# Feed-forward entry of a two-layer hybrid trunk: order of the first products, banks of the conv taps, a fourth plain tile

## The chip, the cores and the metric

One core of a Trainium2 chip runs the whole program in a single launch. The metric is the device time of that launch in microseconds (us), lower is better. The engines that matter are TensorE (PE in the profile, with its weight loads as PEld), VectorE (DVE), ScalarE (ACT), GpSimd (POOL), and the DMA queue that SyncE issues (SP).

## The reference

Two layers over 512 positions and a width of 1024. Each layer adds a mixer (attention of two kinds) and then a feed-forward part to the residual stream; the change sits at the passage from the mixer to the feed-forward part, in both layers.

```python
x = x + mixer(rms_norm(x, norm_mix[i]))        # nsa_mixer, then swa_mixer
h = rms_norm(x, norm_ffn[i])
a, u = jnp.split(h @ w_gu, 2, axis=-1)          # w_gu: 1024 x 5632
a = causal_depthwise_conv(a, conv_w, conv_b)    # three taps along the sequence
x = x + (jax.nn.silu(a) * u) @ w_down           # w_down: 2816 x 1024
```

## The kernel before, in words

Everything is held transposed: 128 features on the partitions, the 512 positions along the free axis. The width of 1024 is eight such tiles, the inner feed-forward width of 2816 is 22 (index f). To keep fp32 accuracy every operand of a product is split into a high part (a cast to fp32r, on ACT) and a low part (the difference, on DVE or POOL), and a product is high times high, high times low and low times high: 24 matmuls of 512 columns for one 128 x 512 result over a width of 1024.

**Leaving the mixer.** `out_last` (L390 to L432) makes the eight tiles of the last quarter of the output projection. For each tile m it adds the product to the residual stream (L421, DVE), splits the result with `split_x` (L300: `xh[m]` on ACT in L305, `xl[m]` on DVE in L306), and two tiles later adds the square of the tile to the statistics of the norm (ACT L232; the sum in L238 on POOL, for the last tiles on DVE). The gain of the norm is in `xh` and `xl`, the factor 1/rms (`rstd`) is not: products can start before it is known, and it is applied to their results.

**First products.** `first_products` (L282) loads the weights of the gate and the up half of f = 0 (`load_w`, L174: DMA to `wraw`, cast to `wh` on ACT in L182, difference `wl` in L183) and makes both products in two PSUM banks, tags `mm` and `s`. Its steps are of three matmuls: for each k the product of the high weight with `xh[k]`, of the high weight with `xl[k]`, of the low weight with `xh[k]`; all eight k of the gate half come before the up half. `finish_among` (L261) puts the reduction of the statistics (L248, L249), the power on POOL (L254) and the transposes that spread the result (L257) among these steps, by the counts in AMONG_FFN.

**Plain tiles.** `gate_up(f)` (L547) runs for f = 0, 1, 2 (PLAIN is 3). It multiplies the gate product by `rstd` into `apad` (L550), runs the three taps and the silu (`activate`, L533: one ACT and two DVE instructions that accumulate in a PSUM bank `py`, then the silu on ACT), makes the up product, multiplies it by `rstd` (L554, DVE) and by the silu (L555, POOL). The gate product is in a bank of tag `mm`, the up product and `py` in banks of tag `s`. There are two banks of `mm`, two of `s`, three of `t` (transposes, and copies that serve as PSUM sources) and one of `o`. The list PLO names the plain halves whose `wl` is made on POOL, by the number 2f + j (j is 0 for gate, 1 for up); the others use DVE.

**Seven-product tiles.** f from the number of plain tiles on is made by `gate_up_7(f)` (L612): a 2 x 2 scheme with seven products of half the columns and half the width (84 matmuls of 256 columns) in place of eight (which is 96). It wants sums and differences of quarters: of the weights (`weights`, L587: four sums on POOL in L596, seven casts on ACT in L602, five copies to `t` banks in L606, seven differences on DVE in L608), made per f, and of the activations (`operands(i)`, L564, for i = 0 to 3), made once per layer into `xs`. One `operands(i)` is two DVE multiplications by the gain and `rstd` (L569), four POOL sums (L573 to L576), four casts on ACT (L579), three copies to `t` banks on ACT (L583) and four differences on DVE (L585). The smallest of the four pieces, `x1l` with 256 columns, has no copy: its difference reads SBUF twice. OPER says after which plain tile each `operands(i)` stands in the program.

**What sets the order.** The program is written tile by tile, and the framework's scheduler puts the instructions of each engine in one order by their place in the program (which is their priority) and by when its own model expects them to be ready; a tag with n buffers is given out in the order of the program. Each engine then runs its list in that order. Weight loads all issue on SP. `issue_after` holds a block of instructions behind one named instruction on the same engine.

Of the kernel before, what the change touches and what calls it, by code (L numbers as in the profile page):

```python
# [11 lines left out]
F32 = mybir.dt.float32  # L12
F32R = mybir.dt.float32r
AF = mybir.ActivationFunctionType
ALU = mybir.AluOpType
AX = mybir.AxisListType

P = 128
T = 512
NT = T // P  # L20
DM = 1024
NK = DM // P
# [9 lines left out]
B_MM, B_S, B_T, B_O = 2, 2, 3, 1  # L32
# [12 lines left out]
LAST = (("mm", "mm", "s", "s", "mm", "mm", "s", "s"),) * 2  # L45
HALVES = slice(0, T // 2), slice(T // 2, T)
STATS_LAG = 2
FULL_NSA = (0, 3)
FULL_SWA = (0, 1, 2, 3, 7)
OUT_ORDER = (6, 2, 0, 1, 7, 3, 4, 5)  # L50
# [4 lines left out]
RATE_NSA = (4.2, 2.8, 1.5, 2.2)  # L55
AMONG_FFN = ((11, 2, 1), (11, 2, 1))
STATS_DVE = (5, 5)
PLAIN = (3, 3)
OPER = ((0, 1, 1, 1), (0, 1, 1, 1))
PLO = ((3, 6, 7), (3, 6))  # L60
BUFS = dict(a1=2, a2=2, u1=2, u2=2, s1=2, s4=2, ha1=2, la1=2, ha2=1, la2=1, hs1=1, ls1=1, hs4=1, ls4=1, hu2=1, lu2=1)
GL = [n for n in ("u1", "a1", "u2", "a2", "s1", "s4", "ha1", "la1", "ha2", "la2", "hs1", "ls1", "hs4", "ls4") for _ in range(BUFS[n])]
BANKS = (0, 1, 3, 5, 4)
# [6 lines left out]
def run(steps):  # L70
    for _ in steps:
        pass
# [67 lines left out]
def trunk(ctx: ExitStack, tc: tile.TileContext, x, w_nsa, w_gate, w_c1, w_c2, w_nsao, w_nsao3, w_swa, w_swao,  # L140
          w_swao3, w_gu, w_dn, consts, tables, vecs, convs, pe, swa_vb, out):
    nc = tc.nc
# [5 lines left out]
    ps = ctx.enter_context(tc.tile_pool(name="ps", bufs=2, space=PSUM))  # L148
# [8 lines left out]
    V = VecIndex(vec)  # L157
# [5 lines left out]
    xh = [cp.tile([P, T], F32R, name=f"xh{k}", tag=f"xh{k}") for k in range(NK)]  # L163
    xl = [cp.tile([P, T], F32R, name=f"xl{k}", tag=f"xl{k}") for k in range(NK)]
# [3 lines left out]
    def f32(t):  # L168
        return t.bitcast(F32)
# [112 lines left out]
    def first_products(layer, stats):  # L282

        ws = [chunks(load_w(w_gu[layer, j, 0], DM, nc.vector), NK) for j in range(2)]
        pts = [ps.tile([P, T], F32, name=n, tag=n, bufs=b) for n, b in (("mm", B_MM), ("s", B_S))]

        def steps():
            for pt, w in zip(pts, ws):
                for k in range(NK):
                    nc.tensor.matmul(pt, w[k][0], xh[k], start=k == 0, stop=False)  # L290
                    nc.tensor.matmul(pt, w[k][0], xl[k], start=False, stop=False)
                    nc.tensor.matmul(pt, w[k][1], xh[k], start=False, stop=k == NK - 1)
                    yield

        s = steps()
        stats.finish_among(s, AMONG_FFN[layer][:2], after=AMONG_FFN[layer][2])
        run(s)
        return pts

    def split_x(xt, k, gain, eng=None):  # L300
        g = V(gain, k)
        if eng is nc.vector:
            ins = nc.vector.tensor_scalar(xh[k], xt, g, None, op0=ALU.mult)
        else:
            ins = nc.scalar.activation(xh[k], xt, AF.Copy, scale=g)  # L305
        nc.vector.scalar_tensor_tensor(xl[k], xt, g, f32(xh[k]), op0=ALU.mult, op1=ALU.subtract)  # L306
        return ins


    def evacuate(pool, pt):  # L310
# [79 lines left out]
    def out_last(out, src, gain, stats, layer):  # L390

        early, (oh, ol) = EARLY[layer], out
        ws, pts = [], {}

        def product(m, c, n, lo, cols=slice(0, T), first=False, last=False):
            o = c * 4 * P + m % 4 * P
            nc.tensor.matmul(pts[m][:, cols], ws[m // 4][n][:, o:o + P], (ol if lo else oh)[:, c, cols],
                             start=first, stop=last)

        def products_0(m):  # L400
            if m % 4 == 0:
                ws.append(next_w())
            tag = LAST[layer][m]
            pts[m] = ps.tile([P, T], F32, name=tag, tag=tag, bufs={"mm": B_MM, "s": B_S, "t": B_T}[tag])
            product(m, 0, 0, 0, first=True)
            product(m, 0, 1, 0)
            product(m, 0, 0, 1)

        for m in range(early):
            products_0(m)  # L410
        for cols in HALVES:
            for m in range(early):
                product(m, 1, 0, 0, cols)
                product(m, 1, 1, 0, cols)
        for m in range(NK):
            if m >= early:
                products_0(m)
                product(m, 1, 0, 0)
                product(m, 1, 1, 0)
            product(m, 1, 0, 1, last=True)  # L420
            nc.vector.tensor_tensor(X[m], pts.pop(m), src[m], op=ALU.add)  # L421
            ins = split_x(X[m], m, gain)
            if m >= STATS_LAG:
                if m - STATS_LAG >= STATS_DVE[layer]:
                    stats.eng = nc.vector
                with tc.issue_after(ins.ins):
                    stats.add(X[m - STATS_LAG], m - STATS_LAG)
        with tc.issue_after(ins.ins):
            for m in range(NK - STATS_LAG, NK):
                if m >= STATS_DVE[layer]:  # L430
                    stats.eng = nc.vector
                stats.add(X[m], m)  # L432

    def out_weights(wa, gs):
        n = 2 * len(gs) * P
# [17 lines left out]
    X, Xt = [None] * NK, [None]  # L453
# [52 lines left out]
def ffn(tc, layer, e):  # L506
    nc, wp, ps, V = e["nc"], e["wp"], e["ps"], e["V"]
    rstd, X, load_w, mm3, proj = e["rstd"], e["X"], e["load_w"], e["mm3"], e["proj"]
    f32, Stats, residual = e["f32"], e["Stats"], e["residual"]
    e["lo_eng"][0] = nc.vector  # L510
    H = T // 2
    with tc.tile_pool(name=f"ffn{layer}", bufs=1) as pool:
# [7 lines left out]
        g, x_tags = {}, [(x, k) for x in ("xh", "xl") for k in range(NK)]  # L520
# [9 lines left out]
        for t in apad:  # L530
            nc.vector.memset(t[:, 0:2], 0.0)

        def activate(f, a):  # L533
            y = pool.tile([P, T], F32, name="y", tag="y", bufs=1)
            py = ps.tile([P, T], F32, name="s", tag="s", bufs=B_S)
            nc.scalar.activation(py, a[:, 2:], AF.Identity, scale=conv(f * 3 + 2), bias=conv(3 * NF + f))
            nc.vector.scalar_tensor_tensor(py, a[:, 1:T + 1], conv(f * 3 + 1), py, op0=ALU.mult, op1=ALU.add)
            nc.vector.scalar_tensor_tensor(py, a[:, 0:T], conv(f * 3), py, op0=ALU.mult, op1=ALU.add)
            nc.scalar.activation(y, py, AF.Silu)
            return y  # L540
# [6 lines left out]
        def gate_up(f):  # L547
            pa = plain(f, 0, "mm") if f else e["first"][0]
            a = apad[f % 2]
            nc.vector.tensor_tensor(a[:, 2:], pa, rstd, op=ALU.mult)  # L550
            y = activate(f, a)
            pu = plain(f, 1, "s") if f else e["first"][1]
            u = gated(f)
            nc.vector.tensor_tensor(u, pu, rstd, op=ALU.mult)  # L554
            nc.gpsimd.tensor_tensor(u, u, y, op=ALU.mult)  # L555
# [3 lines left out]
        xs = pool.tile([P, 7, NK // 2, 2, H], F32R, name="xs")  # L559
# [4 lines left out]
        def operands(i):  # L564
            n = [half(t, F32) for t in (("ha2", "hs4"), ("la2", "ls4"))[i % 2]]
            t = [half(t, F32).rearrange("p (o t) -> p o t", o=2) for t in (("hs1", "hu2"), ("ls1", "lu2"))[i % 2]]
            for h in range(2):
                k = i + h * NK // 2
                nc.vector.scalar_tensor_tensor(n[h], X[k], V(f"ffn{layer}", k), prs, op0=ALU.mult, op1=ALU.mult)  # L569
            x1l, x1r, x2l, x2r = (n[h][:, c] for h in range(2) for c in HALVES)  # L570
            t2, t1, t3, t4 = (t[j][:, h] for j in range(2) for h in range(2))
            eng = nc.gpsimd
            eng.tensor_tensor(t1, x1r, x1l, op=ALU.subtract)  # L573
            eng.tensor_tensor(t3, x2r, x1r, op=ALU.subtract)
            eng.tensor_tensor(t2, x2r, t1, op=ALU.subtract)
            eng.tensor_tensor(t4, x2l, t2, op=ALU.subtract)  # L576
            for o, src in ((slice(0, 1), x1l.unsqueeze(1)), (slice(5, 7), n[1].rearrange("p (o t) -> p o t", o=2)),
                           (slice(1, 3), t[0]), (slice(3, 5), t[1])):
                nc.scalar.copy(xs[:, o, i, 0], src)  # L579
                if o.stop - o.start == 2:  # L580

                    src2 = ps.tile([P, T], F32, name="t", tag="t", bufs=B_T).rearrange("p (o t) -> p o t", o=2)
                    nc.scalar.copy(src2, src)  # L583
                    src = src2
                nc.vector.tensor_tensor(xs[:, o, i, 1], src, f32(xs[:, o, i, 0]), op=ALU.subtract)  # L585

        def weights(f):  # L587
# [23 lines left out]
        def gate_up_7(f, cue):  # L611
            ws = weights(f)  # L612
# [12 lines left out]
            a, u = apad[f % 2], gated(f)  # L625
# [20 lines left out]
            product(pc, 4)  # L646
            add(ul, pc, ul)
            cue(6)
            nc.gpsimd.tensor_tensor(u, u, activate(f, a), op=ALU.mult)

        prs = ps.tile([P, T], F32, name="o", tag="o", bufs=B_O)
        nc.scalar.copy(prs, rstd)
        for f in range(PLAIN[layer]):
            gate_up(f)
# [35 lines left out]
        gain = "mix1" if layer == 0 else None  # L690
# [37 lines left out]
        ins = down(last, halves[1])  # L728
# [5 lines left out]
def nsa(tc, e):  # L734
# [55 lines left out]
    vc = pool.tile([P, 2, P], F32R, name="vc")  # L790
    NV = 4 if max(FULL_NSA, default=0) > 3 else 2
    vcd = pool.tile([P, NV, 2, P], F32R, name="vcd")
# [187 lines left out]
    def head(g, r, fill):  # L980
        q, kk, v2 = qs[g], keys[g], vs[g]
        h = 4 * g + r
        full = h // 2 in FULL_NSA
        pts, acc = {}, []
# [580 lines left out]
```

## Time and profile before

| what | us |
|---|---|
| three timed runs, median (lowest to highest) | 1279.53 (1273.96 to 1279.56) |
| the profiled execution, its own time | 1280.34 |
| its span from first to last instruction | 1278.6 |
| PE busy / DVE / ACT / POOL in the span | 1220.3 / 906.8 / 797.4 / 580.0 |

The profiled execution lies 0.8 us above the median of the timed runs, and 1.7 us of it are outside the span. A row of the timeline has the start, the time from the start to the end of the merged instructions, the engine, the line, the operation, the tiles (out<-in), the shape and the count; a bracket is the engine's idle time just before it and what ended it. A matmul's own duration overlaps the next one's, so a pace is read from starts. The granted clock (PEclk) is a share of full speed.

### The profile page before, as it was taken

To read this page: it belongs to the slowest core of one execution; us is meant where nothing else is said; L and a number is where in the kernel's file an instruction comes from. 1 tells how busy PE (TensorE), PEld (TensorE's weight loads), DVE (VectorE), ACT (ScalarE), POOL (GpSimd) and SP (SyncE) were. 2 spreads that over 40 slices of the span, in tenths; PEclk is the share of its full clock that TensorE was granted. 3 is DMA by queue.
4 is the path that set the end of the run, shared out by engine and by line. 5 is a ranking of instruction groups with operands and counts; after the bars stand their busy time and mean duration, and the time that the engine had idled before them with its cause. 6 is when DMAs were issued, how large, how long until landed. Compare 5 with 4: busy or idle time off the path is not lost.

```text
span 1278.6 us, 20545 instructions
## 1 busy us (share of the span) xinstructions
PE 1220.3 (95%) x7246; PEld 1055.7 (83%) x7246; DVE 906.8 (71%) x1799; ACT 797.4 (62%) x1660; POOL 580.0 (45%) x451
## 2 busy tenths in 40 slices
PE   7999999989998999999999998999889999999997
PEld 5867886777876999999888886778679999998886
DVE  6466777878678888889533367997888788893223
ACT  4377677867549888878422225865687888873222
POOL 4485544533239666764000136322576766620002
PEclk9999999989999999999999999999999999999998
DMA  5746645041122333331233355323423333213323
GB/s 188 229 148 203 195 128 151 30 144 38 49 90 96 116 103 101 106 108 54 85 96 91 107 162 158 111 80 92 133 74 101 99 100 107 87 61 98 100 91 124
DMA packets 66486, 141.71 MB, mean 111 GB/s; under 512 B 8528, under 2 KB 16976, under 8 KB 66384
## 3 DMA queue, kind: packets, MB, share of 16 engines
q1 hardware_dynamic: 65008, 139.25, 35.2%
q8 instruction: 57, 0.93, 0.3%
q10 hardware_dynamic: 1376, 1.15, 0.3%
q14 instruction: 45, 0.37, 0.1%
HBM read 123.14 MB, written 17.24 MB: 110 GB/s over the span
## 4 chain that ended last, share of the span: by engine, by line
PE 67%; DVE 13%; POOL 6%; DMA 5%; issue 5%; ACT 2%; SPq 1%; POOLq 0%; DVEq 0%; ACTq 0%
PE mm L205 29%; PE mm L619 11%; PE s L619 8%; PE o L619 7%; PE s L1165 2%; PE o L1007 1%; PE t L1189 1%; DVE ls L608 1%; PE o L1307 1%; DVE xl L306 1%; DMA q<-d 1%; DMA d<-rh 1%; DVE p L1184 1%; PE t L1409 1%; DMA d<-rl 1%
## 5 line engine op out<-in xcount | busy, mean ns | idle before, releaser
L182 ACT CAST wh<-wraw 128x1024 fp32r<-128x1024 f32 (+3 forms) x132 | 122.2, 926 | 234.9 <-PE mm L205 142.9
L183 DVE TENSOR_TENSOR wl<-wraw,wh 128x1024 fp32r<-128x1024 f32 (+3 forms) x80 | 100.0, 1253 | 115.6 <-PE mm L205 74.8
L183 POOL TENSOR_TENSOR wl<-wraw,wh 128x1024 fp32r<-128x1024 f32 (+3 forms) x52 | 99.0, 1906 | 135.0 <-PE mm L205 67.5
L205 PE MATMUL mm<-xs,wh 128*128 128x512 f32 (+1 forms) x374 | 141.7, 383 | 1.6 <-DVE apad L623 1.6
L238 POOL TENSOR_TENSOR rt<-rt 128x512 f32<-128x512 f32 x22 | 31.5, 1431 | 198.2 <-ACT rt L232 198.0
L205 PE MATMUL mm<-xh,wh 128*128 128x512 f32 x248 | 104.4, 423 | 12.3 <-ACT wh L182 11.3
L205 PE MATMUL mm<-xl,wh 128*128 128x512 f32 x248 | 101.8, 412 | 2.6 <-DVE xl L306 2.6
L608 DVE TENSOR_TENSOR ls<-s,hs 128x512 fp32r<-128x512 f32 x76 | 89.9, 1190 | 3.1 <-ACT hs L602 1.9
L205 PE MATMUL mm<-xs,wl 128*128 128x512 f32 (+1 forms) x374 | 90.9, 382 | 0.0
L619 PE MATMUL o<-xs,ha 128*128 128x256 f32 x608 | 87.2, 287 | 2.2 <-DVE ls L569 1.7
L619 PE MATMUL mm<-xs,hs 128*128 128x256 f32 x608 | 87.8, 283 | 0.3 <-DVE apad L623 0.3
L596 POOL TENSOR_TENSOR s<-u,u 128x512 f32<-128x512 f32 x38 | 51.7, 1361 | 78.6 <-DMA u<-in_w_gu 58.6
L205 PEld LDWEIGHTS mm<-xs,wh 128*128 128x128 f32 x374 | 70.3, 188 | 17.0 <-DVE apad L623 2.0
L1175 ACT ACTIVATE p<-p,sm 128x128 f32<-128x128 f32 (+3 forms) x128 | 71.7, 562 | 19.2 <-DVE sm L1172 18.7
L619 PEld LDWEIGHTS o<-xs,ha 128*128 128x128 f32 x608 | 79.9, 195 | 2.8 <-DVE ls L569 2.1
L205 PEld LDWEIGHTS mm<-xs,wl 128*128 128x128 f32 x374 | 67.7, 188 | 15.2
L619 PEld LDWEIGHTS mm<-xs,hs 128*128 128x128 f32 x608 | 79.2, 191 | 0.6 <-DVE apad L623 0.5
L205 PEld LDWEIGHTS mm<-xh,wh 128*128 128x128 f32 x248 | 49.7, 200 | 25.8 <-ACT wh L182 12.6
L1172 DVE CUSTOM_DVE_ANT_0 p<-s,cst 128x128 f32<-128x128 f32 (+3 forms) x128 | 58.3, 480 | 15.3 <-PE t L1189 8.5
L205 PE MATMUL mm<-xh,wl 128*128 128x512 f32 x248 | 67.1, 400 | 0.0
L602 ACT CAST wh<-wraw 128x512 fp32r<-128x512 f32 x76 | 46.7, 620 | 29.2 <-POOL wraw L596 22.6
L596 POOL TENSOR_TENSOR wraw<-a,u 128x512 f32<-128x512 f32 x38 | 59.4, 1563 | 6.5 <-DMA a<-in_w_gu 3.4
(363 smaller groups left out, 3608.2 us busy)
## 6 DMA issues: line engine op xcount, KB each, us to landing
u<-in_w_gu SPq DMA_DIRECT2D x76, 256.0 KB, 2.6
a<-in_w_gu SPq DMA_DIRECT2D x76, 256.0 KB, 2.6
wraw<-in_w_dn SPq DMA_DIRECT2D x34, 512.0 KB, 3.4
wraw<-in_w_nsa SPq DMA_DIRECT2D x19, 512.0 KB, 5.2
q<-d SPq DMA_DIRECT2D x32, 256.0 KB, 5.2
wraw<-in_w_dn SPq DMA_DIRECT2D x17, 384.0 KB, 3.0
wraw<-in_w_gu SPq DMA_DIRECT2D x12, 512.0 KB, 3.5
d<-rh SPq DMA_DIRECT2D x21, 256.0 KB, 2.2
```

Of the source, the lines that this page charges most:

```text
L182: nc.scalar.copy(wh[:, c], raw[:, c])
L183: (eng or lo_eng[0]).tensor_tensor(wl[:, c], raw[:, c], f32(wh[:, c]), op=ALU.subtract)
L205: nc.tensor.matmul(pt, ws[k][w], rs[k][r], start=first and i == 0, stop=last and i == len(ops) - 1, **kw)
L238: self.eng.tensor_tensor(self.acc, self.acc, sq, op=ALU.add)
L306: nc.vector.scalar_tensor_tensor(xl[k], xt, g, f32(xh[k]), op0=ALU.mult, op1=ALU.subtract)
L596: nc.gpsimd.tensor_tensor(out, x, y, op=op)
L602: nc.scalar.copy(ws[o][0], w)
L608: nc.vector.tensor_tensor(ws[o][1], w, f32(ws[o][0]), op=ALU.subtract)
L619: nc.tensor.matmul(pt, ws[o][w][:, i * P:(i + 1) * P], xs[:, o, i, x], start=start and n == 0, stop=n == len(ops) - 1, skip_group_check=True)
L1165: ins = nc.tensor.matmul(dst, ql, kk[:, :, :n] if shared else kk[:, br, :n], start=c.start == 0 and kk is kst[0], stop=kk is kst[-1], skip ...
L1172: nc.vector.tensor_tensor_reduce(pt[:, c], pss[:, c], mask[:, T - (c.stop - c.start):], -1.0, 3e38, ALU.add, ALU.min, st[:, u:u + 1])
L1175: nc.scalar.activation(pt[:, c], pt[:, c], AF.Exp, scale=-1.0, bias=st[:, u:u + 1], accum_out=st[:, 2 + u:3 + u])
```

## The change

- `split_x` is divided into `split_high` and `split_low`. `out_last` makes the low part of tile m - 3 at tile m (LOW_LAG is 3), and the last three low parts after the statistics.
- `first_products` first makes, for the gate half and then for the up half, the eight products of the high weights with `xh` and the eight of the low weights with `xh`; then for both the eight of the high weights with `xl`. A step is still three matmuls, and the counts that place the statistics among them stay.
- The taps of a plain tile (`py`) take a bank of tag `t`; those of a seven-product tile stay in `s`.
- PLAIN goes from 3 to 4 in both layers: f = 3 becomes a plain tile. The numbers 6 and 7 in PLO, which are its two halves, put both its `wl` on POOL (layer 1 gets the 7 that it lacked). `operands(3)` moves behind the plain tile 2, `operands(1)` and `operands(2)` stay behind 1, `operands(0)` behind 0.
- `operands` copies `x1l` to a `t` bank too, and all four differences read PSUM for one source.

```diff
+LOW_LAG = 3
...
-PLAIN = (3, 3)
-OPER = ((0, 1, 1, 1), (0, 1, 1, 1))
-PLO = ((3, 6, 7), (3, 6))
+PLAIN = (4, 4)
+OPER = ((0, 1, 1, 2), (0, 1, 1, 2))
+PLO = ((3, 6, 7), (3, 6, 7))
...
         def steps():
-            for pt, w in zip(pts, ws):
-                for k in range(NK):
-                    nc.tensor.matmul(pt, w[k][0], xh[k], start=k == 0, stop=False)
-                    nc.tensor.matmul(pt, w[k][0], xl[k], start=False, stop=False)
-                    nc.tensor.matmul(pt, w[k][1], xh[k], start=False, stop=k == NK - 1)
+            order = [(j, x, k) for xs in ((0, 1), (2,)) for j in range(2) for x in xs for k in range(NK)]
+            for i, (j, x, k) in enumerate(order):
+                nc.tensor.matmul(pts[j], ws[j][k][x % 2], (xh, xl)[x // 2][k], start=x == 0 and k == 0,
+                                 stop=x == 2 and k == NK - 1)
+                if i % 3 == 2:
                     yield
...
-            ins = split_x(X[m], m, gain)
+            ins = split_high(X[m], m, gain)
+            if m >= LOW_LAG:
+                split_low(X[m - LOW_LAG], m - LOW_LAG, gain)
...
+        for m in range(NK - LOW_LAG, NK):
+            split_low(X[m], m, gain)
...
-        def activate(f, a):
+        def activate(f, a, tag, bufs):
             y = pool.tile([P, T], F32, name="y", tag="y", bufs=1)
-            py = ps.tile([P, T], F32, name="s", tag="s", bufs=B_S)
+            py = ps.tile([P, T], F32, name=tag, tag=tag, bufs=bufs)
...
-            y = activate(f, a)
+            y = activate(f, a, "t", B_T)
...
                 nc.scalar.copy(xs[:, o, i, 0], src)
-                if o.stop - o.start == 2:
-
-                    src2 = ps.tile([P, T], F32, name="t", tag="t", bufs=B_T).rearrange("p (o t) -> p o t", o=2)
-                    nc.scalar.copy(src2, src)
-                    src = src2
+                src2 = ps.tile([P, T], F32, name="t", tag="t", bufs=B_T).rearrange("p (o t) -> p o t", o=2)
+                src2 = src2[:, :o.stop - o.start]
+                nc.scalar.copy(src2, src)
+                src = src2
                 nc.vector.tensor_tensor(xs[:, o, i, 1], src, f32(xs[:, o, i, 0]), op=ALU.subtract)
...
-            nc.gpsimd.tensor_tensor(u, u, activate(f, a), op=ALU.mult)
+            nc.gpsimd.tensor_tensor(u, u, activate(f, a, "s", B_S), op=ALU.mult)
```

## Rows read from the trace of the kernel before

**Rows 1.** Stretches: us, busy PE, PEld, DVE, ACT, POOL, PEclk, DMA share, GB/s.

```profile
365.40:382.00 16.60, 14.33 (x70) 10.87 (x69) 13.38 (x19) 7.46 (x11) 5.47 (x5) 1.00 0.25 70
382.00:411.00 29.00, 25.30 (x110) 20.61 (x109) 24.31 (x34) 25.19 (x45) 27.78 (x26) 0.94 0.33 108
411.00:420.00 9.00, 6.77 (x41) 5.85 (x40) 8.49 (x13) 8.05 (x17) 3.72 (x4) 0.88 0.25 76
...
500.00:600.00 100.00, 99.17 (x828) 98.85 (x827) 84.99 (x137) 80.58 (x154) 62.84 (x45) 1.00 0.31 97
```

**Rows 2.** Waits of PE, layer 0, 365 to 422 us: total, times, longest.

```profile
PE mm L205 <- ACT wh L182: 3.1, 1, 3.1
PE s L292 <- DVE wl L183: 1.3, 1, 1.3
PE s L619 <- DVE xs L585: 0.8, 1, 0.8
```

**Rows 3.** The longest of the same view in layer 1, 897 to 955 us.

```profile
PE mm L205 <- ACT wh L182: 2.4, 1, 2.4
```

**Rows 4.** Short stretches of both layers, PE alone: us, busy, PEclk, DMA share, GB/s.

```profile
390.60:394.10 3.50, 3.42 (x8) 0.52 0.19 77
...
417.50:421.60 4.10, 4.00 (x21) 0.58 0.57 183
...
922.30:926.50 4.20, 4.20 (x11) 0.59 0.19 73
```

**Rows 5.** Timeline of PE in layer 0, where the parts of the stage begin.

```profile
381.94 0.39 PE L205 MATMUL mm<-xh,wh 128*128 128x512 f32 x1
...
385.56 1.97 PE L205 MATMUL mm<-xh,wl 128*128 128x512 f32 x8
390.68 0.80 PE L205 MATMUL mm<-xh,wh 128*128 128x512 f32 x1 [3.14 <-ACT wh L182]
...
395.98 0.39 PE L205 MATMUL s<-xh,wh 128*128 128x512 f32 x1
...
411.07 0.28 PE L619 MATMUL mm<-xs,wh 128*128 128x256 f32 x1
...
425.91 1.12 PE L619 MATMUL s<-xs,hu 128*128 128x256 f32 x8
...
427.35 1.12 PE L619 MATMUL mm<-xs,hs 128*128 128x256 f32 x8
```

**Rows 6.** Timeline of DVE at the end of layer 0's mixer.

```profile
369.97 0.68 DVE L421 TENSOR_TENSOR X<-s,kl 128x512 f32<-128x512 f32 x1
370.57 1.71 DVE L183 TENSOR_TENSOR wl<-wraw,wh 128x1024 fp32r<-128x1024 f32 x1
```

**Rows 7.** Timeline of ACT in layer 0's plain tiles.

```profile
383.53 0.78 ACT L536 ACTIVATE s<-apad,conv_t 128x512 f32<-128x512 f32 x1 [2.15 <-DVE la L569]
...
389.59 1.04 ACT L182 CAST wh<-wraw 128x1024 fp32r<-128x1024 f32 x1
...
392.98 0.60 ACT L539 ACTIVATE y<-s 128x512 f32<-128x512 f32 x1
...
393.76 0.79 ACT L536 ACTIVATE s<-apad,conv_t 128x512 f32<-128x512 f32 x1
```

**Rows 8.** Timeline of POOL in layer 0's plain tiles.

```profile
385.37 2.40 POOL L183 TENSOR_TENSOR wl<-wraw,wh 128x1024 fp32r<-128x1024 f32 x1 [0.84 <-ACT wh L182]
...
410.15 1.30 POOL L596 TENSOR_TENSOR s<-a,wraw 128x512 f32<-128x512 f32 x1
411.41 0.76 POOL L576 TENSOR_TENSOR lu<-ls,ls 128x256 f32<-128x256 f32 x1
```

**Rows 9.** Timeline of DVE beside it.

```profile
385.62 2.42 DVE L585 TENSOR_TENSOR xs<-ha,xs 128x256 fp32r<-128x256 f32 x1 [0.23 <-ACT xs L579]
...
388.57 0.41 DVE L585 TENSOR_TENSOR xs<-la,xs 128x256 fp32r<-128x256 f32 x1
...
415.07 0.68 DVE L585 TENSOR_TENSOR xs<-t,xs 128x512 fp32r<-128x512 f32 x1
```

More of the change, by code (lines that the diff above doesn't have):

```diff
@@ L300, in split_x, with split_high, split_low @@
     def split_x(xt, k, gain, eng=None):
-        g = V(gain, k)
+        ins = split_high(xt, k, gain, eng)
+        split_low(xt, k, gain)
+        return ins
+    def split_high(xt, k, gain, eng=None):
         if eng is nc.vector:
[L303 to L307, printed above, removed]
+            return nc.vector.tensor_scalar(xh[k], xt, V(gain, k), None, op0=ALU.mult)
+        return nc.scalar.activation(xh[k], xt, AF.Copy, scale=V(gain, k))
+    def split_low(xt, k, gain):
+        nc.vector.scalar_tensor_tensor(xl[k], xt, V(gain, k), f32(xh[k]), op0=ALU.mult, op1=ALU.subtract)
     def evacuate(pool, pt):
```

## The prediction
> **What bounds the kernel now.** I read the busy times by stretch first. In the settled part of the seven-product tiles PE is busy 99.17 of 100 us [rows 1]: TensorE sets the end there, and time that PE loses earlier is not made up later. The same view then shows where it is lost: PE is idle for 2.3 us of the 16.6 us of the first products (16.60 - 14.33), for 3.7 of the 29.0 us of the plain tiles (29.00 - 25.30) and for 2.2 of the 9.0 us in which the seven-product tiles start (9.00 - 6.77) [rows 1]. The waits of PE name who was late: `wl` and `xl` on DVE in the first, the cast of `wh` for 3.1 us in the second, differences on DVE in the third [rows 2]; layer 1 has the same pattern with a longest wait of 2.4 us [rows 3]. The granted clock adds to it: after the long wait it is 0.52 over 3.5 us, after the waits at the start of the seven-product tiles 0.58 over 4.1 us [rows 4]. Those are the two levels of 1.2 and 2.4 GHz mixed; at a share of 0.52 a stretch loses 0.48 of its length.
>
> Last I read the timelines for the reason of the long wait. The gate product of f = 1 runs from 381.94, with 16 matmuls up to 385.56, so 0.226 us each; its last eight end their turn at 387.4. Then comes the gate of f = 2 at 390.68, and the up half of f = 1 only at 395.98 [rows 5]. Its low weights were ready at 387.8 (385.37 + 2.40) [rows 8], so weights did not hold it. Its bank did: the silu that frees the first tap bank ends at 393.6, and the next tap, which stands before the up product in the program, takes a bank at 393.76 [rows 7].
>
> **The change, part by part.** Times are against the profiled execution, 1280.34 us, which stands 0.8 us above the median of the timed runs.
>
> *First products.* 48 matmuls before and after, 48 x 0.226 = 10.8 us of PE [rows 5]; only the waits can go. Before, the adds that make the last tiles of X stand behind `xl` work on DVE, the last at 369.97, and the second `wl` behind it at 370.57 for 1.71 us [rows 6]. After, 32 matmuls (7.2 us) need no `xl`. But DVE does the same work, 13.38 us in a stretch of 16.6 [rows 1], and the second `wl` is now wanted after 24 matmuls and stands behind the last low parts in the program. Bounds: all of the 2.3 us gained, or as much lost, if PE waits for that `wl` instead. I take 1.5 us per layer, nearer to the gain, as half the slack of the old order was the adds that now go first: **-3.0 us**. The statistics keep their counts, and `rstd` comes as much earlier. Weight slots: the high gate weights are now held for 40 matmuls instead of 24, so the cast for f = 1 starts 8 x 0.226 = 1.8 us before its product; it takes 1.04 us [rows 7], and that is covered.
>
> *Tap banks.* With the taps out of `s`, the up half of f = 1 follows the gate half at once. That removes the 3.3 us from 387.4 to 390.68 and the slow clock behind it, 3.5 x 0.48 = 1.7 us; in layer 1 2.4 us and 4.2 x 0.41 = 1.7 us [rows 3, 4]. Next could be late the cast of `wh` for f = 2, done at 390.6 before [rows 7]: PE now wants it after two halves of 24 matmuls from 380.4, at 391.3, so it may stay where it is. Sum: **-9.1 us**, bounds -9.1 and 0.
>
> *Fourth plain tile and the operands.* PE: 48 x 0.226 = 10.8 us for the tile instead of 84 matmuls of 256 columns; 12 of them take 427.35 - 425.91 = 1.44 us [rows 5], so 10.1 us. **+0.8 us** per layer, **+1.6 us** in all, and PE has no cover for it. What it buys is time for POOL, DVE and ACT before the first seven-product tile. Loss at that start before: 0.6 us of the plain stretch (3.7 less the long wait of 3.1) [rows 1, 2], 2.2 us, and 4.1 x 0.42 = 1.7 us of clock [rows 1, 4], so 4.5 per layer, 9.0 in all (layer 1 taken alike).
> The chain runs over POOL, busy 27.78 of 29.0 us [rows 1]: its last operand sum runs to 412.2 [rows 8] and the last difference of the operands to 415.75 [rows 9], 4.7 us after PE's first seven-product matmul at 411.07 [rows 5]. After, PE arrives at 380.4 + 3 x 10.8 = 412.8. On POOL come two `wl` of 2.40 us, 4.8 together; before the last operand sum go the four sums of one seven-product tile, 4 x 1.30 = 5.2 us [rows 8], as one tile less is due by then. So POOL ends that chain between 410.3 (all of it moves, and `rstd` is 1.5 earlier) and 415.5 (the scheduler still puts two tiles' sums ahead), and the last difference comes 1.1 to 6.3 us after PE's arrival, against 4.7 before. DVE gets no `wl` from f = 3 and ends the two-source differences of `x1l`. I take 7.5 of the 9.0 us as gained, the end where the sums move, since they are the lowest in priority; bounds +9.0 and -2.6: **-7.5 us**.
>
> *Copies of `x1l`.* Four more ACT copies of 256 columns a layer; a cast of 1024 columns takes 1.04 us [rows 7], so by estimate 0.3 us each. ACT is busy 25.19 of 29.0 us [rows 1], so its idle time covers them, and without it they cost 1.2 us a layer. The trace shows what they avoid: the difference of `x1l` took 2.42 us beside a POOL instruction of 2.40, and 0.41 when alone [rows 8, 9]. The Trainium skill, "SBUF — State Buffer", section "SBUF: two separate sides", has an exclusive lock there: a VectorE operation with two SBUF inputs and a GpSimd operation do not share, the later one waits for the whole of the other. The trace agrees with it in these two rows. By that rule the two new `wl` on POOL speak against the change: each could hold a two-source difference of DVE for up to 2.4 us, and if all of it came on the chain the sum would be 9.6 us worse.
>
> *DMA and SP.* The weights of f = 3 are 1 MB either way, as two loads in place of four; they queue on SP ahead of the next tile's, and no PE wait in these rows is for a load.
>
> Sum: 1280.3 - 3.0 - 9.1 - 7.5 + 1.6 = **1262 us**.
>
> **The rivals.**
> - *POOL stays the bound.* The two `wl` go before the operand sums without the other sums moving out, and the start of the seven-product tiles loses 1.3 us more per layer than now. For it: POOL has 1.2 us to spare in 29 [rows 1]. Against it: the displaced 5.2 us. 1280.3 - 3.0 - 9.1 + 2.6 + 1.6 = 1272 us, up to 1280 if each of the four `wl` of both layers also holds a difference on the chain for 2.0 us (2.42 - 0.41) [rows 8, 9].
> - *It was weights, not banks.* The up half of f = 1 starts no earlier and the 9.1 us stay: 1271 us. Against it: `wl` at 387.8 and the start at 395.98 [rows 5, 8].
> - *Taps hold the transposes' banks* (slower). The first tap holds its bank from 383.53 to 393.6, 10.1 us [rows 7], and there are three `t` banks, given out in program order. If the operand copies behind the taps of f = 0 and 1 wait for both, 20 us, the last difference comes at 415.75 - 1.5 + 20.2 = 434.5; less the 4.7 us after arrival that are there now, PE waits 17 us where it lost 4.5. Per layer -1.5 - 4.5 + 12.5 + 0.8 = +7: 1295 us. It decides from about 10 us of such waiting per layer. Against it: two banks stay free, and a difference of 512 columns that frees a bank takes 0.68 us [rows 9].
>
> **How the numbers follow.** The forecast has 0.62, POOL as the bound 0.20, weights instead of banks 0.08, the tap banks 0.07, and 0.03 are left for no effect by a reordering elsewhere. A measurement of this kernel tells 0.5% from no change, 6.4 us, so faster means below 1273: the forecast, the second rival and half of the first, 0.80; same is the other half and the rest, 0.13; slower 0.07. The range: all gains at their ends give 1280.3 - 4.6 - 9.1 - 9.0 + 1.6 = 1259; restarts after waits, which busy time hides, and half of the spread of the timed runs put the low end at 1254; the first rival's price puts the high end at 1273.
>
> **What would show it.** Right: the up half of f = 1 directly behind its gate half, no wait over 1 us of PE on `wh`; the first `xl` product after 32 others; a granted clock above 0.9 from the first products to the second seven-product tile; PE at its first seven-product matmul about 47 us after the first product, against 45.7 now, with one tile more done. Wrong: PE waits on `wl` in the first products, waits of several us on `xs` or `ls` with POOL busy before them, or copies to `t` banks standing behind a silu.

## The result and the profile after

The kernel after takes 1269.1 us (median of 13 runs, 1259.4 to 1275.9) against 1280.2 us before (13 runs, 1274.0 to 1287.2): a ratio of **0.9907 [0.9883, 0.9931]**, about 11 us faster. The profiled execution after took 1271.48 us, with a span of 1269.6.

The stretches of layer 0 again, with the columns of [rows 1]:

```profile
365.40:382.00 16.60, 14.46 (x71) 11.20 (x71) 12.43 (x18) 7.43 (x12) 5.52 (x5) 1.00 0.12 38
382.00:411.00 29.00, 29.00 (x130) 24.01 (x129) 23.61 (x37) 26.34 (x47) 27.14 (x24) 1.00 0.45 155
411.00:420.00 9.00, 6.62 (x41) 5.82 (x40) 8.02 (x6) 4.95 (x10) 6.99 (x7) 1.00 0.16 58
500.00:600.00 100.00, 98.06 (x816) 97.45 (x815) 87.04 (x139) 81.59 (x155) 59.68 (x43) 1.00 0.28 92
```

PE is busy for all 29.0 us of the plain tiles, where it lost 3.7 before, and the granted clock there is 1.00 where it was 0.94. At the start of the seven-product tiles the slow clock is not gone, only later: the stretch up to 420 us shows 1.00, but behind the wait of 2.38 us (below) the granted clock is 0.57 over 3.8 us, as it was 0.58 over 4.1 us before [rows 4]. PE alone, in the columns of [rows 4]:

```profile
419.70:423.50 3.80, 3.71 (x18) 0.57 0.00 0
```

The first products hardly changed (14.46 busy against 14.33), and in the settled part PE is busy a little less than before, 98.06 of 100 us. The waits of PE in layer 0 from 365 to 430 us (total, times, longest):

```profile
PE s L629 <- DVE xs L595: 2.4, 1, 2.4
PE mm L292 <- ACT xh L310: 1.7, 2, 0.9
PE o L629 <- ACT apad L639: 0.8, 1, 0.8
PE s L292 <- DVE X L427: 0.4, 1, 0.4
```

The wait of 3.1 us on the cast of `wh` [rows 2] is gone. In the first products `wl` and `xl` have given way to `xh` and `X`. The longest wait is now for a difference on DVE at the start of the seven-product tiles. In PE's timeline the parts begin here:

```profile
381.73 0.39 PE L206 MATMUL mm<-xh,wh 128*128 128x512 f32 x1
...
385.36 1.98 PE L206 MATMUL mm<-xh,wl 128*128 128x512 f32 x8
387.17 0.39 PE L206 MATMUL s<-xh,wh 128*128 128x512 f32 x1
...
412.56 1.11 PE L629 MATMUL o<-xs,ha 128*128 128x256 f32 x8
...
419.79 0.39 PE L629 MATMUL s<-xs,wh 128*128 128x256 f32 x1 [2.38 <-DVE xs L595]
420.02 1.48 PE L629 MATMUL mm<-xs,hs 128*128 128x256 f32 x7
```

The up half of f = 1 follows its gate half at 387.17 without a gap; before it came at 395.98 [rows 5]. The first seven-product matmul starts at 412.56, 47.1 us after the first product at 365.47; nine of them run before the last eight matmuls of f = 3, which end their turn at 415.45. What holds it up 4 us later is seen in DVE's timeline:

```profile
413.04 6.10 DVE L618 TENSOR_TENSOR ls<-s,hs 128x512 fp32r<-128x512 f32 x2 [0.63 <-POOL lu L586]
419.06 0.68 DVE L595 TENSOR_TENSOR xs<-t,xs 128x512 fp32r<-128x512 f32 x1
```

and in POOL's beside it:

```profile
412.96 1.30 POOL L606 TENSOR_TENSOR wraw<-s,a 128x512 f32<-128x512 f32 x1
414.21 1.29 POOL L606 TENSOR_TENSOR wraw<-a,u 128x512 f32<-128x512 f32 x1
415.46 1.29 POOL L565 TENSOR_TENSOR g<-g,y 128x512 f32<-128x512 f32 x1
416.71 1.28 POOL L606 TENSOR_TENSOR s<-a,wraw 128x512 f32<-128x512 f32 x1
```

Two differences `ls`, each with both operands in SBUF, took 6.10 us. The view by line splits them (count, then nanoseconds as shortest/median/longest); the two have their mean in the middle:

```profile
L618 DVE TENSOR_TENSOR ls<-s,hs x2: 679/3090/5501, 413.0 to 418.5; 128x512 fp32r<-128x512 f32 x2
```

The first lasted 5.50 us, until POOL's row of four operations was through, and the `xs` for which PE waits stood behind it. The copy that this `xs` reads had been on ACT from 413.56 for 0.59 us, so it could have run from 414.15. The shorter of the two is 0.68 us.

**A ledger of what PE loses.** To compare kernels by stage I take the start times of PE's matmuls in the trace. The time from one start to the next, less the pace of the first matmul (0.2267 us for 512 columns, 0.1197 for 256, as they follow each other at full clock), is lost time, a wait or a slow clock alike; the short matmuls of the statistics are left out. Summed over the two layers' feed-forward, in us, with "start" the first 180 seven-product matmuls:

| profile | first products | plain tiles | start | settled tiles | sum |
|---|---|---|---|---|---|
| before | 7.0 | 9.3 | 12.4 | 8.5 | 37.1 |
| after | 6.4 | 0.0 | 8.1 | 9.4 | 23.9 |

The sum falls by 13.2 us; the fourth plain tile adds 1.6 us of work by these paces, so the ledger says -11.6 us; the runs say -11 by the medians and -12 by the ratio.

### The profile page after: what moved, and what is told of

Its sections match the earlier page's. It is cut to its first block, busy times and chain, and to the rows that moved or that the text cites. A ratio compares the mean times of both kernels' runs of the same rounds, so it can differ in the third digit from the quotient of the medians.

```text
span 1269.6 us, 20326 instructions
## 1 busy us (share of the span) xinstructions
PE 1217.9 (96%) x7174; PEld 1051.2 (83%) x7174; DVE 899.4 (71%) x1779; ACT 790.2 (62%) x1644; POOL 575.7 (45%) x447
## 4 chain that ended last, share of the span: by engine, by line
PE 73%; DVE 13%; issue 4%; POOL 4%; DMA 4%; ACT 2%; SPq 0%; POOLq 0%; DVEq 0%; ACTq 0%
PE mm L206 31%; PE mm L629 11%; PE s L629 8%; PE o L629 7%; PE s L1175 2%; PE s L206 2%; PE t L1199 2%; DVE ls L618 2%; PE o L1017 1%; DVE xl L313 1%; PE o L1317 1%; DVE p L1194 1%; DMA q<-d 1%; DMA d<-rl 1%; PE t L1419 1%
## 5 line engine op out<-in xcount | busy, mean ns | idle before, releaser
L183 ACT CAST wh<-wraw 128x1024 fp32r<-128x1024 f32 (+3 forms) x136 | 126.4, 930 | 244.0 <-PE mm L206 149.7
L184 POOL TENSOR_TENSOR wl<-wraw,wh 128x1024 fp32r<-128x1024 f32 (+3 forms) x56 | 108.5, 1940 | 135.4 <-PE mm L206 70.6
L206 PE MATMUL mm<-xh,wh 128*128 128x512 f32 x264 | 108.4, 412 | 7.1 <-ACT wh L183 5.1
L206 PE MATMUL mm<-xl,wh 128*128 128x512 f32 x264 | 106.0, 403 | 2.1 <-DVE xl L313 2.1
L618 DVE TENSOR_TENSOR ls<-s,hs 128x512 fp32r<-128x512 f32 x72 | 94.3, 1320 | 2.6 <-POOL lu L586 1.3
L629 PE MATMUL o<-xs,ha 128*128 128x256 f32 x576 | 81.0, 283 | 1.8 <-ACT apad L639 1.8
L629 PEld LDWEIGHTS o<-xs,ha 128*128 128x128 f32 x576 | 74.3, 192 | 2.4 <-ACT apad L639 2.2
L206 PE MATMUL mm<-xh,wl 128*128 128x512 f32 x264 | 71.7, 402 | 0.0
L206 PEld LDWEIGHTS mm<-xl,wh 128*128 128x128 f32 x264 | 51.0, 194 | 13.7 <-DVE xl L313 4.5
L450 DVE TENSOR_TENSOR X<-mm,X 128x512 f32<-128x512 f32 (+1 forms) x25 | 16.6, 667 | 62.9 <-PE mm L206 62.7
```

The source lines that it names most:

```text
L183: nc.scalar.copy(wh[:, c], raw[:, c])
L184: (eng or lo_eng[0]).tensor_tensor(wl[:, c], raw[:, c], f32(wh[:, c]), op=ALU.subtract)
L206: nc.tensor.matmul(pt, ws[k][w], rs[k][r], start=first and i == 0, stop=last and i == len(ops) - 1, **kw)
L450: ins = nc.vector.tensor_tensor(dst, pt, src, op=ALU.add)
L618: nc.vector.tensor_tensor(ws[o][1], w, f32(ws[o][0]), op=ALU.subtract)
L629: nc.tensor.matmul(pt, ws[o][w][:, i * P:(i + 1) * P], xs[:, o, i, x], start=start and n == 0, stop=n == len(ops) - 1, skip_group_check=True)
```

## The experiments

The time of each is given as its ratio to the kernel before, measured beside it, with a 95% interval, and as that ratio's difference from 1, times 1281 us. Ledger numbers are sums over both layers, as above.

**Tap banks alone**, on the kernel before:

```diff
-        def activate(f, a):
+        def activate(f, a, tag, bufs):
...
-            py = ps.tile([P, T], F32, name="s", tag="s", bufs=B_S)
+            py = ps.tile([P, T], F32, name=tag, tag=tag, bufs=bufs)
...
-            y = activate(f, a)
+            y = activate(f, a, "t", B_T)
...
```

> The kernel before with one edit: the taps of the plain tiles in t banks, three plain tiles as before. Parts add up (the forecast's ledger): the long wait of PE at f = 1 goes in both layers and the time falls by about 9 us, to a ratio near 0.993. Cover theory: PE then reaches the seven-product tiles about 5 us earlier while POOL and DVE finish the operands when they did, so the waits at that start grow by about as much, the sum of PE's losses per layer stays near 14 us, and the time falls by less than 3 us.

1.0018 [0.9995, 1.0042], +2 us. The plain tiles lose nothing any more (9.3 to 0.0), and the start loses 25.0 instead of 12.4. The two longest waits of PE there, in layer 0, are now these:

```profile
PE s L619 <- ACT xs L579: 3.3, 1, 3.3
PE o L619 <- DVE la L608: 2.1, 1, 2.1
```

The long wait in the plain tiles was time in which POOL, ACT and DVE made the operands of the seven-product tiles. Without it PE arrives earlier and waits for them there. The term was real, and alone it is worth nothing, as the cover theory had it.

**The fourth tile without the tap banks**, on the kernel after:

```diff
-            y = activate(f, a, "t", B_T)
+            y = activate(f, a, "s", B_S)
```

> The changed kernel with the taps of plain tiles back in s banks. If the bank held the up half of f = 1: the long wait of 2 to 3 us with the slow clock behind it is back at f = 1 in both layers, and the time is 8 to 10 us above the changed kernel, near that of the kernel before. If weights held it: no wait comes back at f = 1 and the time stays within 2 us of the changed kernel.

0.9993 [0.9971, 1.0015], -1 us. The long wait is back in its place, and a little longer than the 3.1 us of before:

```profile
PE mm L206 <- ACT wh L183: 4.0, 1, 4.0
```

The plain tiles lose 11.2, and the start only 0.3, since PE has cover twice over. The settled tiles lose 16.3 against 9.4; that part I have not traced to a cause.

**Three plain tiles**, on the kernel after:

```diff
-PLAIN = (4, 4)
-OPER = ((0, 1, 1, 2), (0, 1, 1, 2))
+PLAIN = (3, 3)
+OPER = ((0, 1, 1, 1), (0, 1, 1, 1))
```

> The changed kernel with three plain tiles and all operands but the first behind tile 1. Parts add up: 1.6 us faster from the cheaper tile, less what is lost at the start of the seven-product tiles, 7.5 us by the forecast, so about 6 us slower than the changed kernel. Cover theory: PE waits for operand differences at the start of f = 3 by 8 us or more per layer with the slow clock behind it, and most of the gain over the kernel before is lost (slower than the changed kernel by 7 to 11 us).

1.0067 [1.0039, 1.0096], +9 us, some 20 us slower than the kernel after. The start loses 30.0, in waits of this kind:

```profile
PE s L629 <- ACT xs L589: 2.9, 1, 2.9
PE mm L629 <- ACT xs L589: 1.9, 1, 1.9
PE o L629 <- DVE la L618: 1.5, 1, 1.5
```

So the banks alone give +2 us, the rest of the change without the banks -1 us, and the rest without the tile +9 us: only with tile and banks together do the 11 us come. The two were not run as a pair without the other parts of the change.

**The old order in the first products**, on the kernel after:

```diff
-LOW_LAG = 3
+LOW_LAG = 0
...
-            order = [(j, x, k) for xs in ((0, 1), (2,)) for j in range(2) for x in xs for k in range(NK)]
+            order = [(j, x, k) for j in range(2) for k in range(NK) for x in (0, 2, 1)]
...
```

> The changed kernel with the old entry: low parts made at once, three products per k in turn. Forecast's term: slower than the changed kernel by 3 us. What the trace after the change suggests: DVE made its adds and low parts in the same order as before, so the entry is worth 0.3 us per layer and the time is within 1 us of the changed kernel, with the waits of PE again on wl and xl in place of xh.

0.9921 [0.9894, 0.9949], -10 us: not to be told from the kernel after, nor do these intervals shut out the 3 us of the forecast. The waits for `wl` (1.3) and `xl` (0.7) come back where those for `xh` and `X` were. In the profiled execution, the slowest of its five (1275.3 us, median 1269.0), the first products lose 10.1 us where the kernel before lost 7.0 with the same waits. The rest is the clock. PE alone after the wait of 1.3 us, this kernel in layer 0 and then the kernel before:

```profile
373.20:376.80 3.60, 3.52 (x9) 0.54 0.42 146
...
372.30:375.90 3.60, 3.56 (x16) 1.00 0.47 146
```

So by waits alone the new order is worth 0.6 us, and up to 3.7 us in an execution whose clock falls there. DVE's timeline of the kernel after shows why it is not more:

```profile
366.19 0.68 DVE L427 TENSOR_TENSOR X<-mm,kh 128x512 f32<-128x512 f32 x1
366.79 1.17 DVE L313 SCALAR_TENSOR_TENSOR xl<-X,vec,xh 128x512 fp32r<-128x512 f32 x1
...
368.48 1.65 DVE L313 SCALAR_TENSOR_TENSOR xl<-X,vec,xh 128x512 fp32r<-128x512 f32 x1
370.05 0.68 DVE L427 TENSOR_TENSOR X<-s,kl 128x512 f32<-128x512 f32 x1
370.64 1.70 DVE L184 TENSOR_TENSOR wl<-wraw,wh 128x1024 fp32r<-128x1024 f32 x1
```

The last add runs at 370.05 and the second `wl` at 370.64; before it was 369.97 and 370.57 [rows 6]. The order written in the program moved the low parts by three tiles, and DVE still does them between the adds.

**The low parts really behind the last add**, on the kernel after:

```diff
+        with tc.issue_after(stats.last_add):
+            for m in range(NK):
+                split_low(X[m], m, f"ffn{layer}")
...
-            nc.vector.tensor_tensor(X[m], pts.pop(m), src[m], op=ALU.add)
+            stats.last_add = nc.vector.tensor_tensor(X[m], pts.pop(m), src[m], op=ALU.add).ins
...
-            if m >= LOW_LAG:
-                split_low(X[m - LOW_LAG], m - LOW_LAG, gain)
...
-        for m in range(NK - LOW_LAG, NK):
-            split_low(X[m], m, gain)
```

> The kernel after, with all low parts of the first products behind the last add that makes X, and the low parts of the weights where the first products ask for them. Theory (low parts between the adds make the last tiles of X late): the adds of X4 to X7 end some 4 us earlier, and what TensorE loses in the first products falls from 3.2 to about 1 us a layer, so about 1265 us. Rival (VectorE has too much to do in these 16.6 us whatever the order, 13.4 us of it): the wait only moves to xl and wl behind the adds, the loss stays between 2.5 and 4 us a layer, and the time within 2 us of the kernel after.

0.9911 [0.9882, 0.9941], -11 us, the same as after. The last add is four us earlier, at 366.06, but the first products lose 8.4 instead of 6.4, in these waits of PE:

```profile
PE s L295 <- DVE wl L184: 1.7, 1, 1.7
PE s L295 <- ACT wh L183: 1.0, 1, 1.0
```

The rival holds (4.2 us a layer, just above its 4): in this stretch DVE has 12.43 us of work in 16.6 in the kernel after, and another order only changes which result PE waits for. That the amount of DVE's work is what sets the loss is the likeliest reading; no run here made that work less.

**Copies to PSUM for the first seven-product tile's weights**, on the kernel after:

```diff
-                if o in BANKS:
+                if o in BANKS or f == PLAIN[layer]:
```

> The kernel after, with all seven weights of the first seven-product tile copied to PSUM before their difference is formed, where now some of the differences read two SBUF operands. Theory (a difference of VectorE with two SBUF inputs is held while GpSimd works through several operations, 5.5 us in layer 0 of the profile after): that long difference is gone, the loss at the start of the seven-product tiles falls from 5.2 to 2 or 3 us in layer 0 and little in layer 1, so 1265 to 1267 us. Rival (ScalarE is the one that is late there): the added copies of 0.6 us each make the loss the same or 1 us more per layer, 1269 to 1271 us.

0.9868 [0.9835, 0.9900], -17 us. The start loses 2.4 instead of 8.1, and the wait of 2.4 us on `xs` is gone; behind the entry the longest wait of PE in layer 0 is this one:

```profile
PE o L629 <- ACT apad L639: 0.7, 1, 0.7
```

The two added copies hurt nothing. The order of POOL's work moved in this kernel too, so this run alone doesn't separate the hold from its surroundings.

**No copies of `x1l`**, on the kernel after:

```diff
-                src2 = src2[:, :o.stop - o.start]
-                nc.scalar.copy(src2, src)
-                src = src2
+                if o.stop - o.start == 2:
...
+                    nc.scalar.copy(src2, src)
+                    src = src2
```

> The kernel after without the copies of the single-half operand, whose four differences a layer then read two SBUF operands again. Theory (such a difference is held by GpSimd): these differences grow from about 0.4 to between 1.3 and 2.4 us and the start of the seven-product tiles loses 1 to 4 us more a layer, 1271 to 1277 us. Rival (the copies only load ScalarE): the time is the same or 1 to 2 us shorter, 1267 to 1269 us, with four copies fewer a layer.

0.9954 [0.9930, 0.9979], -6 us, about 5 us slower than the kernel after, with the two intervals just touching. The differences by line in layer 0, in the form of the view above:

```profile
L595 DVE TENSOR_TENSOR xs<-ha,xs x2: 754/800/845, 387.1 to 396.3; 128x256 fp32r<-128x256 f32 x2
L595 DVE TENSOR_TENSOR xs<-la,xs x2: 406/676/947, 389.0 to 402.2; 128x256 fp32r<-128x256 f32 x2
```

With copies four such took 0.42 us each (1.7 us in all). They grow by 0.3 us on average, less than I had put down, and the start loses 9.1 against 8.1. The larger part, 15.5 against 9.4 in the settled tiles, comes mostly at their end, as one wait a layer. This is the wait in layer 0 in the kernel after, and then in this one:

```profile
PE mm L206 <- DVE apad L633: 1.1, 1, 1.1
...
PE mm L206 <- DVE apad L633: 2.3, 1, 2.3
```

The five-plain kernel below has the copies of `x1l` and waits the same 2.3 us at the same place, so this part is not the missing copies themselves but the order of DVE's work: in both of these kernels two differences `la` (L681, 1.29 us together) stand ahead of the add that PE waits for, and in the kernel after behind it. What the copies are worth by themselves is nearer to the 1.0 us at the start.

**A fifth plain tile**, on the kernel after (`PLAIN = (5, 5)`):

> The kernel after with a fifth plain tile. Theory (four plain tiles already cover the operands, what is left at the start is order and contention): 48 matmuls of 512 columns in place of 84 of 256 cost 0.8 us a layer and the loss at the start falls by at most 1 us, so 1269 to 1272 us. Rival (the chain over GpSimd is still too long): the loss at the start falls from 5.2 and 2.9 us to below 1 us in both layers, so about 6 us less 1.6, 1264 to 1266 us.

0.9916 [0.9884, 0.9948], -11 us. The start falls to 2.1, and the settled tiles rise to 13.4, a good part of it again at their end, with 1.6 us more of work. Neither theory had that: the start did behave nearly as the rival said (1.5 and 0.6 us a layer), the time as the theory.

**Copies for all weights of all tiles, for six of seven, and with the low parts last.** On the kernel after, `BANKS = (0, 1, 2, 3, 4, 5, 6)`; then `BANKS = (0, 1, 3, 5, 4, 2)` with all seven in the first tile; then five of seven, all seven in the first tile, and the low parts last:

> The kernel after, with all seven weights of every seven-product tile copied to PSUM, so that no weight difference reads two SBUF operands. Theory (what helps is order and contention at the first of these tiles alone, where PE has no cover): the start gains as in the run with the copies in that tile alone, the settled tiles lose, since ScalarE gets 34 copies of 0.59 us a layer more, 20 us, on 132 of 160 busy, and the time is 1264 to 1272 us. Rival (the differences that GpSimd holds are what delays PE in the settled tiles too): VectorE's differences fall from 1.1 to 0.7 us each, the waits of about 1 us a tile go, and the time is 1256 to 1261 us.

> The same with six of seven weights in every tile and all seven in the first. Theory: half of the added copies, so between the run with the copies in the first tile alone and the run with all of them, 1264 to 1268 us. Rival (held differences delay the settled tiles): 1259 to 1262 us.

> The kernel after with both the low parts behind the last add and all seven weights of the first seven-product tile copied to PSUM. Theory (the first products lose about 1 us a layer more, the copies gain 3 to 5 us in all as alone): 1262 to 1266 us. Rival (the gain of the copies was a better order of that run's schedule, not the copies): 1267 to 1270 us, as with the low parts alone.

0.9812 [0.9782, 0.9841], -24 us, 1256.5 us; 0.9802 [0.9769, 0.9835], -25 us, 1257.1 us; and 0.9877 [0.9839, 0.9915], -16 us. My theory failed in the first two, and the rival was right (the second came out 2 us below even its range): the held differences cost time in the settled tiles as well. By line, 425 to 610 us, the kernel after:

```profile
L618 DVE TENSOR_TENSOR ls<-s,hs x34: 678/1384/1821, 424.6 to 594.3; 128x512 fp32r<-128x512 f32 x34
L618 DVE TENSOR_TENSOR la<-t,ha x34: 674/680/693, 425.2 to 589.8; 128x512 fp32r<-128x512 f32 x34
```

and with copies for all:

```profile
L618 DVE TENSOR_TENSOR ls<-t,hs x34: 680/681/693, 428.3 to 587.6; 128x512 fp32r<-128x512 f32 x34
```

The same instruction on the same data takes 1.38 us in the median from SBUF and 0.68 from a PSUM bank, with no spread. What PE waited for in that stretch, after:

```profile
PE mm L206 <- DVE apad L633: 1.1, 1, 1.1
PE s L629 <- DVE xh L633: 1.1, 2, 0.8
PE s L629 <- DVE xl L633: 1.1, 2, 0.6
...
```

and with copies for all:

```profile
PE mm L206 <- DVE apad L633: 0.5, 1, 0.5
```

The waits on `xh` and `xl` (tiles that line 633's adds write here) were for adds by which DVE frees a bank. In the kernel after such adds stand in DVE's queue behind the `ls` that are held, as here:

```profile
540.61 2.96 DVE L618 TENSOR_TENSOR ls<-s,hs 128x512 fp32r<-128x512 f32 x2
543.49 0.41 DVE L633 TENSOR_TENSOR xl<-s,apad 128x256 f32<-128x256 f32 x1
```

With the copies no `ls` is held, and these waits are gone. ScalarE pays for it and can:

```profile
500.00:600.00 100.00, 99.48 (x821) 98.82 (x821) 79.57 (x145) 92.30 (x180) 50.83 (x40) 1.00 0.29 88
```

It is 92.30 us busy in 100 instead of 81.59, and DVE 79.57 instead of 87.04. The third kernel, at 1265.2 us, came out as its theory said: it has the gain of the first tile's copies and not more.

**Three plain tiles with the copies** (six of seven weights), to see whether the fourth tile only covered held differences:

> The kernel with the copies of six and seven weights, with three plain tiles in place of four. Theory (the fourth plain tile buys time that the chain of operands over GpSimd, ScalarE and VectorE needs in any case): TensorE loses more than 10 us a layer at the start of the seven-product tiles, as in the run of the kernel after with three plain tiles (16 and 14 us), and the time is 1270 to 1280 us. Rival (that loss was differences held by GpSimd, and the fourth tile only covered them): the loss at the start is below 5 us a layer, the tile's 0.8 us a layer come back, and the time is 1254 to 1260 us.

1.0002 [0.9973, 1.0031], no change from before, and 25 us slower by the ratios than the same kernel with four. The start loses 31.1. PE's longest waits there:

```profile
PE s L629 <- ACT xs L589: 2.7, 1, 2.7
PE mm L629 <- ACT xs L589: 2.1, 1, 2.1
```

and ACT's own, on the sums of POOL:

```profile
ACT xs L589 <- POOL hu L586: 3.4, 1, 3.4
```

POOL has no pause meanwhile: PE's first seven-product matmul here is at 404.30, and POOL works through the weight sums of two tiles and the operand sums up to 414.15. One stretch of it, with the columns of [rows 1]:

```profile
400.00:411.00 11.00, 7.89 (x37) 6.02 (x35) 8.12 (x14) 8.81 (x18) 11.00 (x12) 0.88 0.15 48
```

The chain of the operands over POOL needs the time of the fourth tile whether differences are held or not.

The ledger beside the runs, in us against before, with the work of the plain tiles added (0.8 a tile and layer):

| kernel | start | settled tiles | sum | ledger says | runs say |
|---|---|---|---|---|---|
| tap banks alone | 25.0 | 8.3 | 40.3 | +3 | +2 |
| taps in `s` | 0.3 | 16.3 | 34.2 | -1 | -1 |
| three plain tiles | 30.0 | 10.4 | 46.8 | +10 | +9 |
| after | 8.1 | 9.4 | 23.9 | -12 | -12 |
| old order | 9.7 | 9.3 | 29.1 | -6 | -10 |
| low parts last | 6.8 | 7.1 | 22.3 | -13 | -11 |
| first tile's copies | 2.4 | 9.5 | 18.3 | -17 | -17 |
| no copies of `x1l` | 9.1 | 15.5 | 30.9 | -5 | -6 |
| five plain tiles | 2.1 | 13.4 | 21.9 | -12 | -11 |
| copies for all | 2.0 | 1.3 | 9.7 | -26 | -24 |
| copies for six | 2.5 | 1.9 | 10.7 | -25 | -25 |
| first tile's copies, low parts last | 2.3 | 8.9 | 19.7 | -16 | -16 |
| copies for six, three tiles | 31.1 | 1.8 | 39.3 | +2 | 0 |

The ledger is of one profiled execution, the runs of several. The two last columns agree within 2 us but for the old order, whose profiled execution was the slowest of its five and had a granted clock of 0.54 and 0.58 over 3.6 us of the first products in its two layers; so the time is where the ledger has it.

## Why the prediction was right, and where it was not

The forecast was 1262 us and faster; it is faster, at 1269, inside the range, by 11 us where 18 were forecast. The time by itself decides little, since it lies nearer to the 1272 us of the rival "POOL stays the bound" than to the forecast; the traces tell the two apart. TensorE as the bound holds all through: what it lost or got back by the ledger shows in the time within 2 us, one kernel apart.

- *Tap banks, -9.1.* The ledger has -9.3, the up half of f = 1 is where it was forecast, and undoing this alone brings the wait back. So "it was weights, not banks" is out. But this term stood in the sum as if by itself, and by itself it gives +2 us.
- *Fourth plain tile, +1.6, and the start of the seven-product tiles, -7.5.* Taking the tile away costs 20 us, so it is far more than a small price: it pays for the cover that the tap banks take away. "POOL stays the bound" is out with four tiles and holds with three. The start itself gained 4.3 by the ledger, of 12.4 where the text had 9.0. The chain over POOL came within its bounds: its last operand sum ended at 413.0 (412.27 + 0.73), inside 410.3 to 415.5, with five weight sums ahead of it instead of eight. But the last difference of the operands ended at 419.74, 7.2 us after PE's first seven-product matmul. The step that failed was that "the last difference comes 1.1 to 6.3 us after PE's arrival" with the near end taken, because the sums move. The sums were the smaller trouble, 2.7 us past the end that was taken. The larger one was DVE's `ls`, held for 5.50 us right in front of the difference that PE needed. The text had a hold, of up to 2.4 us and by the two new `wl`; it came from three weight sums and the product of f = 2 with its silu (L565), and was twice as long.
- *First products, -3.0.* Measured -0.6 (7.0 to 6.4, where the text had 4.6 to be lost before). The step that failed is "half the slack of the old order was the adds that now go first". They don't go first: DVE's order is unchanged, and its times to 0.1 us. Where another kernel makes them go first, the loss does not fall but rises, to 8.4. The old order on the kernel after lost 10.1 in one execution, 3.7 more: 0.6 by waits and the rest by a slower clock behind them, and the forecast had put no clock in this term.
- *Taps holding the transposes' banks* (the slower rival). Not seen. In the kernel with the tap banks alone PE loses 32 us from the first product to the end of the start, against 28.6 before, that is under 2 us a layer more, far from the 10 us from which it decides. In layer 0 of the kernel after the one long wait of ACT for a bank of `t` (3.8 us) was for the held difference, not for a silu.
- The settled part lost 0.9 more than before, which no term had: -0.6 - 9.3 - 4.3 + 0.9 + 1.6 = -11.7.
- *The signs.* The up half of f = 1, the missing wait on `wh` and the 47 us came as named. The 47 us are chance: in the kernel before, 13 seven-product matmuls run from 403.24 on, ahead of the up half of f = 2, so 411.07 is the first one behind the plain tiles, and 45.7 and 47.1 us don't measure the same thing. Two signs of being right failed: the first `xl` product came after 24 others instead of 32 (at 373.95), and the clock fell to 0.57 at the start of the seven-product tiles. One sign of being wrong came: the wait on `xs`, 2.4 us, with POOL busy before it.

So the mechanism was right, two terms were too large (2.4 and 3.2 us), and the right sum was not one of independent terms: loss at the start is the helpers' finish less PE's arrival, and both the banks and the tile change the arrival.

## To carry to other kernels

A wait that is removed ahead of a stage fed by other engines only moves PE's arrival: work out that stage's loss from the new arrival, and change the cover in the same step. An order written in the program is no order on an engine until the trace shows it. Where VectorE subtracts two SBUF tiles beside a busy GpSimd, a copy of one operand to PSUM on ScalarE is worth trying even where it brings ScalarE to 92% busy: here it gave 1.0% more, and the version that beats both kernels.

## What the runs showed of the hardware

An operation of DVE with two SBUF inputs can be held through several POOL operations in a row, 5.50 us for an instruction that takes 0.68 alone. In the profiled execution of the old order one took 6.86 us, beside five POOL operations of 1.3 us in a row:

```profile
413.46 6.86 DVE L618 TENSOR_TENSOR ls<-s,hs 128x512 fp32r<-128x512 f32 x1
```

In both it ended within 0.6 us of the end of POOL's row. The pair of `ls` in layer 1 of the kernel after shows the other form:

```profile
L618 DVE TENSOR_TENSOR ls<-s,hs x2: 1767/1775/1783, 944.4 to 946.1; 128x512 fp32r<-128x512 f32 x2
```

There each was held for one POOL operation of about 1.3 us, and POOL's next one in turn took 1.74 us. The Trainium skill, "SBUF — State Buffer", section "SBUF: two separate sides", has it that whoever starts first keeps the ports for its whole instruction and the other blocks. Layer 1 agrees with that, and 0.68 us with one operand in PSUM does too; the 5.50 us of layer 0 goes beyond it, since three further POOL operations started while DVE waited. What decides between the two forms no run here shows.

The waits alone do not settle the clock: after the same waits of 0.7 and 1.3 us in the first products it was 1.00 in the kernel before and 0.54 with the old order on the kernel after. No run here shows why.

The other surprise is how much ScalarE could take: 34 more copies in a layer's settled tiles, two to a tile, raised it to 92.30 us in 100 and PE still gained.
